# The first layer of a two-layer fp32 trunk in another order: S5 tables between attention projections, the output projection in two halves, a contiguous scan state, softmax scaling on ScalarE

## The chip, the core and the metric

The kernel runs on one NeuronCore of a Trainium2 chip. The metric is the device time of one execution in microseconds. Engines are called by short names: PE is TensorE (matmuls and transposes), DVE is VectorE, ACT is ScalarE, POOL is GpSimd, SP is SyncE, which issues most of the DMAs.

## What is computed

One sequence of L = 256 tokens, D = 2048, all in float32. Two layers share a residual stream. Layer 0 ("even") projects its normed input to q, k, v, u, z_A, z_B of 1024 columns each, runs chunked attention on q, k, v and a state-space model (S5) on u, gates both, and adds their common output projection to x. Layer 1 ("odd") is a causal attention with forget gates; the change does not touch it. The core of layer 0 in the reference:

```python
def even_layer(...):
    hn = rmsnorm(x, norm_g)
    proj = hn @ w_in
    q, k, v, u, z_a, z_b = jnp.split(proj, cuts, axis=-1)
    o_a = chunked_relpos_attention(q.reshape(shp), k.reshape(shp), v.reshape(shp), rel_bias)
    o_a = o_a * jax.nn.silu(z_a)
    y = jax.nn.gelu(s5_ssm(u, lam_re, lam_im, log_dt, b_re, b_im, c_re, c_im, d_skip).astype(x.dtype))
    o_b = y * jax.nn.sigmoid(y @ w_glu + b_glu)
    o_b = o_b * jax.nn.silu(z_b)
    return x + jnp.concatenate([o_a, o_b], axis=-1) @ w_out
```

`s5_ssm` computes, for each of 64 groups of 16 channels, a complex state of 64 numbers, x_t = A x_(t-1) + B u_t, and y_t = Re(C x_t) + D u_t. The attention has 16 heads of 64; with 256 tokens each frame sees its own chunk of 64 and the chunks before it, with a bias by distance.

## The kernel before

**Projections.** Every weight is split on the chip into a float32r high part and the remainder. `next_w` (L117 to L135) loads a 512 KB tile `wr` through SP's queue (4 buffers), ACT rounds it to `wh` (L133), DVE subtracts to `wl` (L134); both have 3 buffers and a scheduling priority 3000 places ahead. `project` (L137 to L158) then does, for each block kb of 128 rows and each half of 128 tokens, three matmuls of 128x512 (L144, L145, L146: high by high, high by low, low by high): 12 matmuls for a weight tile, 96 for a projection of 512 columns over 16 blocks. The weight tiles lie in DRAM in the order in which the program asks for them.

**Order.** The code states dependences and a program order; a scheduler in the framework places the instructions of each engine by priority, and each engine then runs its own list in that order. PE's list in layer 0 is: u0, u1 | zb0, za0, za1 | q0, k0, v0 | q1, k1, v1 | zb1 | glu0, glu1 | oe0 to oe3. Attention runs in two halves (hf) of eight heads: `scores` and `probs` per pair of heads (L552 to L565), mixing with v (L578 to L595).

**S5.** Time is cut into 32 chunks (NCH) of 8 steps (TC). `tables(e)` (L317 to L383) makes, for eight groups e = 0 to 7, the input matrix w1, transposed by PE over `pm` to `min`, the output matrix mx, stored to `m_d`, and the kernel matrix ks, stored to `k_d`. Tables 0 to 2 come before u1, the others after it. `pv`, `vs`, `pvt` (L407 to L422) turn u into chunk inputs in X. The scan (L428 to L433) has 30 steps of four DVE operations on 128 numbers per partition; X is `[P, 2, G, 33]`, so neighbours of a step lie 132 bytes apart. `s5_final` (L500 to L539) loads from `k_d` eight pieces per e into T (five on SP's queue, three on POOL's) and from `m_d` one into mo (SP), in 4 buffers shared with `min`; `py` (L516, L520) multiplies u by T and X by mo, ACT applies GELU into yn (L522), yn goes to DRAM as `y_d` and over `pyt` into yTh and yTl. It stands before v0 in the code. `glu` is a projection over 8 blocks; its result, gated, goes transposed (`out_T`) into blocks 8 to 15 of cTh and cTl, the attention's into blocks 0 to 7; oe0 to oe3 project all 16 and add x.

Of the kernel before, what the change touches and what calls it, by code (L numbers as in the profile page):

```python
# [9 lines left out]
F32 = mybir.dt.float32  # L10
# [32 lines left out]
def trunk(ctx: ExitStack, tc: tile.TileContext, a, out: bass.AP):  # L43
# [120 lines left out]
    l0p = l0.enter_context(tc.tile_pool(name="l0p", bufs=1))  # L164
    s5bx, s5ax = ExitStack(), ExitStack()
# [3 lines left out]
    xt = s5b.tile([P, 2, D], F32, name="xt", tag="X")  # L169
    xr = [s5b.tile([P, 8, L], F32, name=f"xTr_{c}", tag=t_) for c, t_ in enumerate(("un", "uT"))]  # L170
    pre = []

    def x_block(kb):
        src = xr[kb // 8][:, kb % 8, :]
        nc.scalar.activation(xTh[:, kb, :], src, AF.Copy, scale=gE[:, kb:kb + 1])
        nc.vector.scalar_tensor_tensor(xTl[:, kb, :], src, gE[:, kb:kb + 1],
                                       xTh[:, kb, :].bitcast(F32), op0=ALU.mult, op1=ALU.subtract)

    for k0, k1 in ((0, 2), (2, 4), (4, 8), (8, 12), (12, 16)):
        nc.sync.dma_start(xr[k0 // 8][:, k0 % 8:k0 % 8 + k1 - k0, :], a["xT"][:, k0:k1, :])  # L180
# [22 lines left out]
    k_d = dram.tile([NGQ, P, 2 * TC * GC], F32, name="k_d")  # L203
# [3 lines left out]
    uts = []  # L207
    for n in range(2):
        if n == 1:
            pre = [next_w() for _ in range(3)]  # L210
            for t in range(2):
                tc.keep_in_program_order(nc.sync.dma_start(xt[:, t, :], xin[:, t, :]))
                pre += [next_w() for _ in range(2)]
            r0, r0q = rms0(xt)
            pre.append(next_w())
            for t in range(2):
                nc.vector.tensor_scalar(uts[t], uts[t], r0[:, t:t + 1], None, op0=ALU.mult)
                nc.sync.dma_start(u_d[t * P:(t + 1) * P, 0:NT], uts[t])
        acc = project(xTh, xTl, 16, f"u{n}", pre)
        for t in range(2):  # L220
            ut = s5b.tile([P, NT], F32, name=f"ut_{n}_{t}", tag="ut", bufs=3)
            uts.append(ut)
            if n == 0:
                nc.scalar.copy(ut, acc[t])
            else:
                nc.scalar.activation(ut, acc[t], AF.Copy, scale=r0[:, t:t + 1])
                nc.sync.dma_start(u_d[t * P:(t + 1) * P, NT:], ut)
        if n == 0:

            def sm(name):  # L230
                return s5.tile([P, G], F32, name=name, tag="sm_" + name)

            lr, li, dt = sm("lr"), sm("li"), sm("dt")
            for h in range(2):
                nc.gpsimd.dma_start(lr[h * 64:(h + 1) * 64, :], a["s5lr"])
                nc.gpsimd.dma_start(li[h * 64:(h + 1) * 64, :], a["s5li"])
            nc.gpsimd.dma_start(dt, a["s5dt"].to_broadcast([P, G]))
            dcol = s5.tile([P, NGQ], F32, name="dcol")
            nc.gpsimd.dma_start(dcol, a["s5d"])

            sgn = s5.tile([P, 1], F32, name="sgn")
            nc.vector.memset(sgn[0:64, :], -1.0)
            nc.vector.memset(sgn[64:128, :], 1.0)
            nsgn = s5.tile([P, 1], F32, name="nsgn")
            nc.vector.memset(nsgn[0:64, :], 1.0)
            nc.vector.memset(nsgn[64:128, :], -1.0)
            ddiag = s5.tile([P, NGQ, GC], F32, name="ddiag")
            dmask = s5.tile([P, GC], F32, name="dmask")
            for g4 in range(4):
                nc.vector.tensor_copy(dmask[32 * g4:32 * g4 + 32, :],  # L250
                                      ident[32 * g4:32 * g4 + 32, 32 * g4:32 * g4 + GC])
            nc.vector.tensor_tensor(ddiag, dmask.unsqueeze(1).to_broadcast([P, NGQ, GC]),
                                    dcol.unsqueeze(2).to_broadcast([P, NGQ, GC]), op=ALU.mult)

# [48 lines left out]
            V.tensor_tensor(ci, pi[:, 1, :], lr, op=ALU.mult)
            V.tensor_tensor(t0, nr, li, op=ALU.mult)
# [560 lines left out]
```

## Time and profile before

| | us |
|---|---|
| median of three runs | 972.3 |
| lowest and highest | 972.21, 973.33 |
| the profiled execution | 975.55 |
| its span, first to last instruction | 973.5 |
| start of layer 1 (first matmul of cq) | 480.4 |

PE is busy for 941.0 us of the span, DVE for 603.9, ACT for 494.4, POOL for 84.5; the mean granted clock of TensorE is 0.988. In views of the trace L134 is line 134 of the kernel, names of tiles stand without the numbers of their buffers, and "A <- B: 3.3, 3, 2.1" in a list of waits means that A waited for B three times, 3.3 us in all, 2.1 at most. A matmul's printed length includes its way through the array; the distance between two starts is what it costs.

### The profile page before, as it was taken

What the parts mean: (1) busy time and instruction counts of PE and PEld (TensorE: products, weight loads), DVE (VectorE), ACT (ScalarE), POOL (GpSimd) and SP (SyncE); (2) the same over time, 40 slices, a digit from 0 to 9 for tenths busy, and PEclk for the clock granted to TensorE, in tenths of its full rate; (3) what the DMA queues carried; (4) which work ended last, traced back from release to release, by engine and by line L of the source; (5) the groups of instructions that cost most, each with busy time, mean ns of one, the idle gap of its engine ahead of it and who ended that gap; (6) DMA issues with size and microseconds to landing.
All of it is one profiled execution on the core that took longest, in us unless ns stands there. A gap on an engine that the chain in (4) does not pass through costs nothing.

```text
span 973.5 us, 13313 instructions
## 1 busy us (share of the span) xinstructions
PE 941.0 (97%) x4828; PEld 758.7 (78%) x4828; DVE 603.9 (62%) x1095; ACT 494.4 (51%) x730; POOL 84.5 (9%) x142
## 2 busy tenths in 40 slices
PE   7999999999997999999999999999999999999996
PEld 5877887776775786788887888888888888888884
DVE  6899989599832668655546445445544554455463
ACT  6635555445452567444544555456445544554451
POOL 2100000100021010000000320011001100100210
PEclk9999999999997999999999999999999999999998
DMA  8788767755599664556664654555455545554562
GB/s 306 282 246 291 236 206 221 200 167 164 164 244 258 211 204 154 174 199 208 198 223 156 213 194 152 195 174 194 153 193 178 169 158 190 180 170 159 190 207 87
DMA packets 72577, 191.47 MB, mean 197 GB/s; under 512 B 7488, under 2 KB 27184, under 8 KB 72128
## 3 DMA queue, kind: packets, MB, share of 16 engines
q1 hardware_dynamic: 71520, 188.93, 60.5%
q0 software_dynamic: 992, 1.69, 0.9%
q8 instruction: 38, 0.62, 0.3%
q14 instruction: 27, 0.22, 0.1%
HBM read 180.09 MB, written 10.50 MB: 196 GB/s over the span
## 4 chain that ended last, share of the span: by engine, by line
PE 79%; DVE 11%; DMA 5%; issue 3%; ACT 1%; SPq 0%; POOL 0%; POOLq 0%; DVEq 0%; ACTq 0%
DVE wl L134 4%; PE acc_oe L145 3%; PE acc_oe L144 3%; PE acc_oe L146 3%; PE acc_cv L144 3%; PE acc_cq L145 3%; PE acc_cq L146 3%; PE acc_cq L144 3%; PE acc_ck L144 3%; PE acc_cv L145 3%; PE acc_cz L145 3%; PE acc_cz L146 3%; PE acc_cz L144 3%; PE acc_cv L146 3%; PE acc_ck L145 3%; PE acc_ck L146 3%
## 5 line engine op out<-in xcount | busy, mean ns | idle before, releaser
L134 DVE TENSOR_TENSOR wl<-wr,wh 128x1024 fp32r<-128x1024 f32 (+1 forms) x292 | 357.3, 1226 | 286.1 <-ACT wh L133 282.4
L133 ACT ACTIVATE wh<-wr 128x1024 fp32r<-128x1024 f32 (+1 forms) x292 | 307.6, 1056 | 302.8 <-PE acc_ck L146 41.8
L145 PE MATMUL acc_cv<-wl,x1Th 128*128 128x512 f32 x128 | 51.0, 399 | 0.0
L146 PE MATMUL acc_cq<-wh,x1Tl 128*128 128x512 f32 x128 | 50.8, 397 | 0.0
L145 PE MATMUL acc_oe<-wl,cTh 128*128 128x512 f32 x128 | 50.8, 398 | 0.0
L145 PE MATMUL acc_cz<-wl,x1Th 128*128 128x512 f32 x128 | 50.7, 396 | 0.0
L146 PE MATMUL acc_cz<-wh,x1Tl 128*128 128x512 f32 x128 | 50.4, 394 | 0.0
L146 PE MATMUL acc_cv<-wh,x1Tl 128*128 128x512 f32 x128 | 50.4, 393 | 0.0
L145 PE MATMUL acc_cq<-wl,x1Th 128*128 128x512 f32 x128 | 50.3, 393 | 0.0
L145 PE MATMUL acc_ck<-wl,x1Th 128*128 128x512 f32 x128 | 50.2, 392 | 0.0
L146 PE MATMUL acc_oe<-wh,cTl 128*128 128x512 f32 x128 | 50.0, 397 | 0.0
L146 PE MATMUL acc_ck<-wh,x1Tl 128*128 128x512 f32 x128 | 49.9, 390 | 0.0
L144 PE MATMUL acc_cq<-wh,x1Th 128*128 128x512 f32 x128 | 48.5, 398 | 0.0
L144 PE MATMUL acc_cz<-wh,x1Th 128*128 128x512 f32 x128 | 48.3, 402 | 0.0
L144 PE MATMUL acc_oe<-wh,cTh 128*128 128x512 f32 x128 | 48.3, 400 | 0.0
L144 PE MATMUL acc_cv<-wh,x1Th 128*128 128x512 f32 x128 | 47.7, 398 | 0.0
L144 PE MATMUL acc_ck<-wh,x1Th 128*128 128x512 f32 x128 | 46.2, 390 | 0.0
L146 PE MATMUL acc_oo<-wh,oTl 128*128 128x512 f32 x108 | 42.2, 391 | 0.0
L145 PE MATMUL acc_oo<-wl,oTh 128*128 128x512 f32 x108 | 42.1, 390 | 0.0
L144 PE MATMUL acc_oo<-wh,oTh 128*128 128x512 f32 x108 | 39.8, 393 | 0.0
L724 POOL TENSOR_SCALAR cbt<-ckb,cum 128x128 f32<-128x128 f32 x16 | 10.3, 642 | 328.8 <-DVE mx_c L473 271.0
L144 PE MATMUL acc_u<-wh,xTh 128*128 128x512 f32 x64 | 23.8, 412 | 6.3 <-ACT wh L133 6.3
(391 smaller groups left out, 2025.5 us busy)
## 6 DMA issues: line engine op xcount, KB each, us to landing
wr<-in_w_dram SPq DMA_DIRECT2D x295, 512.0 KB, 3.5
m_d<-mx SPq DMA_DIRECT2D x8, 512.0 KB, 4.5
mo<-m_d SPq DMA_DIRECT2D x8, 512.0 KB, 7.0
T<-k_d SPq DMA_DIRECT2D x40, 64.0 KB, 5.6
bc<-in_s5bc_dram SPq DMA_DIRECT2D x8, 256.0 KB, 5.0
xt<-in_x_dram SPq DMA_DIRECT2D x2, 1024.0 KB, 9.4
k_d<-ks SPq DMA_DIRECT2D x8, 256.0 KB, 3.3
bt<-in_rbx_dram SPq DMA_DIRECT2D x8, 256.0 KB, 4.4
```

Source lines behind the costliest of these rows:

```text
L133: nc.scalar.activation(wh[:, c], raw[:, c], AF.Copy)
L134: nc.vector.tensor_tensor(wl[:, c], raw[:, c], wh[:, c].bitcast(F32), op=ALU.subtract)
L144: nc.tensor.matmul(acc[t], sh, wh[:, c], start=kb == 0, stop=False)
L145: nc.tensor.matmul(acc[t], sh, wl[:, c], start=False, stop=False)
L146: nc.tensor.matmul(acc[t], sl, wh[:, c], start=False, stop=kb == nkb - 1)
L724: W.tensor_scalar(bt[:, 0, :], ckb[:, hh, 0:P], cum[:, 0, h:h + 1], None, op0=ALU.add)
```

## The change

1. Layer 0's program order becomes u0, u1, q0, k0, v0, za0, q1, k1, v1, za1, zb0, zb1, with one `tables(e)` and one pair of heads placed after each projection or two. The scan starts behind zb0. The weight tiles in DRAM follow the new order.
2. The output projection is split by its input: oa0 to oa3 (8 blocks, attention half, aTh and aTl) run before the S5 output is complete and add x into tiles xa_n; oe0 to oe3 (8 blocks, S5 half, bTh and bTl) add xa_n at the end.
3. X is `[P, 33, 2, G]`: the 128 numbers of one step are contiguous.
4. In `probs` of layer 0 the scaling by the reciprocal sum and the copy pT go from DVE to ACT; so do the half swaps of vs.
5. Tables: bb and its companion are made in three operations of 256 elements in place of six of 128; slot 0 of w1 and of mx is copied by ACT, DVE computes the other 7 and 8. `k_d` has another layout and is written by four DMAs per e.
6. All loads of T and mo are on POOL's queue, in 7 buffers; `y_d` is written in two halves.

The core of the diff:

```diff
-    X = s5b.tile([P, 2, G, NCH + 1], F32, name="X")
-    nc.gpsimd.memset(X[:, :, :, 0:1], 0.0)
+    X = res.tile([P, NCH + 1, 2, G], F32, name="X", tag="X")
+    nc.gpsimd.memset(X[:, 0], 0.0)
...
+        for n in range(1, NCH - 1):
+            V.tensor_tensor(st2, e2, X[:, n, ::-1, :], op=ALU.mult)
+            V.tensor_tensor(st1, e1, X[:, n], op=ALU.mult)
+            V.tensor_tensor(st2, st2, X[:, n + 1], op=ALU.add)
+            V.tensor_tensor(X[:, n + 1], st1, st2, op=ALU.add)
...
+        V.tensor_tensor(bb, bc[:, :, 0:2, :],
+                        cr[:, sl].unsqueeze(2).unsqueeze(3).to_broadcast([P, 8, 2, GC]), op=ALU.mult)
...
+        nc.scalar.copy(w1[:, :, 0, :], bb[:, :, 0, :])
+        V.tensor_tensor(w1[:, :, 1:8, :], pw(pr, up), wide(bb[:, :, 0, :], 7), op=ALU.mult)
...
-        nc.vector.tensor_copy(vs[:, 1, :, 0:64], pv[:, :, 64:128])
-        nc.vector.tensor_copy(vs[:, 1, :, 64:128], pv[:, :, 0:64])
+        nc.scalar.copy(vs[:, 1, :, 0:64], pv[:, :, 64:128])
+        nc.scalar.copy(vs[:, 1, :, 64:128], pv[:, :, 0:64])
...
-            nc.vector.tensor_scalar(lg[:, 0, :], lg[:, 0, :], rs[:, 0:1], None, op0=ALU.mult)
-            nc.vector.tensor_scalar(lg[:, 1:3, :], lg[:, 1:3, :], rs[:, 1:2], None, op0=ALU.mult)
+            nc.scalar.activation(lg[:, 0, :], lg[:, 0, :], AF.Copy, scale=rs[:, 0:1])
+            nc.scalar.activation(lg[:, 1:3, :], lg[:, 1:3, :], AF.Copy, scale=rs[:, 1:2])
...
-        nc.vector.tensor_copy(pT, pp)
+        if scaled:
+            nc.scalar.copy(pT, pp)
...
-                (nc.gpsimd if j % 8 >= 5 else nc.sync).dma_start(
...
-            nc.sync.dma_start(mo, m_d[e])
+            tt_ = s5c.tile([P, 8, P], F32, name=f"T_{e}", tag="TM", bufs=7)
...
+                nc.gpsimd.dma_start(tt_[j * GC:(j + 1) * GC], k_d[e, :, :, GC * (j + 1):GC * (j + 1) + P])
...
+            nc.gpsimd.dma_start(mo, m_d[e])
...
+    a0.proj("q", r0q)
+    tables(0)
+    a0.proj("k", r0)
+    tables(1)
+    a0.pair(0)
+    a0.proj("v", r0)
+    tables(2)
+    a0.pair(1)
+    a0.gate()
+    tables(3)
...
+    scan()
+    a1.pair(1)
+    a1.mix(0)
+    a1.mix(1)
+    zb.append(gate("zb1"))
+    for hp in (2, 3):
+        a1.pair(hp)
+        a1.mix(hp)
...
+    def out_a(n):
+        t_ = at.tile([P, 2, NT], F32, name=f"xa_{n}", tag=("qk", "qk", "v", "za")[n], bufs=(2, 2, 1, 3)[n])
+        nc.sync.dma_start(t_, xin[:, :, n * NT:(n + 1) * NT])
+        acc = project(aTh, aTl, 8, f"oa{n}")
+        for t in range(2):
+            V.tensor_tensor(t_[:, t, :], acc[t], t_[:, t, :], op=ALU.add)
+        xa.append(t_)
+
+    out_a(0)
+    yns = s5_final()
+    out_a(1)
+    yT = res.tile([P, 2, 8, L], F32R, name="yT", tag="X")
+    s5_y(yns, yT[:, 0], yT[:, 1])
...
-        acc = project(cTh, cTl, 16, f"oe{n}")
...
+        acc = project(bTh, bTl, 8, f"oe{n}")
```

`pair(hp)` is the body of the old loop over pairs of heads (transposes of q and k, scores, `probs`), `mix(i)` the old product with v with og, aTh and aTl, `gate` the old projection with SiLU.

The order of DVE's instructions shows where the scan lies. Before, its steps stand among the weight splits of k0 to k1 and the softmax of the first heads (st1 and st2 are the two temporaries, wl_67 is a weight tile of q1, a2 a head):

```order
L430 TENSOR_TENSOR st2_1235<-e2_431,X_806 128x128
L431 TENSOR_TENSOR st1_1234<-e1t_434,X_806 128x128
L432 TENSOR_TENSOR st2_1235<-st2_1235,X_806 128x128
L134 TENSOR_TENSOR wl_67_2868<-wr_67_2866,wh_67_2867 128x1024
L433 TENSOR_TENSOR X_806<-st1_1234,st2_1235 128x128
L471 ISA lg_a2_2203,mx_a2_2204<-psc_a2_2197,bt_0_1_2194 128x128
```

Now its last steps stand behind the splits of zb1 and of the first part of oa1 (a15 is the last head, og_1_3 the last attention output, xa_0 the sum of oa0 with x, wl_102 the third weight tile of oa1):

```order
L435 TENSOR_TENSOR st1_2896<-e1t_215,X_655 128x128
L482 RECIPROCAL rs_a15_3346<-sm_a15_3343 128x2
L436 TENSOR_TENSOR st2_2897<-st2_2897,X_655 128x128
L437 TENSOR_TENSOR X_655<-st1_2896,st2_2897 128x128
L558 TENSOR_TENSOR og_1_3_3361<-poa_1_3_3356,zaT_1_2510 128x256
L560 TENSOR_TENSOR aTl_107<-og_1_3_3361,aTh_106 128x256
L654 TENSOR_TENSOR xa_0_3365<-acc_oa0_0_3367,xa_0_3365 128x512
L654 TENSOR_TENSOR xa_0_3365<-acc_oa0_1_3368,xa_0_3365 128x512
L134 TENSOR_TENSOR wl_102_3727<-wr_102_3725,wh_102_3726 128x1024
```

The scan moved from the middle of layer 0 to just ahead of the S5 output, and the split wl_102 is queued behind its end. On PE, before, the S5 output is followed by the end of v1 and by zb1 (pyt are the transposes of y, poa the attention outputs of the first half):

```order
L590 MATMUL poa_2_2791<-pT_a_2293,v_2624 64x128
L146 MATMUL acc_v_0_3324<-wh_3453,xTl 128x512
L144 MATMUL acc_v_1_3325<-wh_3453,xTh 128x512
L145 MATMUL acc_v_1_3325<-wl_3454,xTh 128x512
L146 MATMUL acc_v_1_3325<-wh_3453,xTl 128x512
L144 MATMUL acc_zb_0_3508<-wh_3511,xTh 128x512
```

Now py_0 and its neighbours stand between the last head and the end of oa0 (acc_oa_0 and acc_oa_1 are the two token halves):

```order
L488 MATMUL pp_a_3331<-ident,lg_a_3318 128x128 x3
L552 MATMUL poa_3_3356<-pT_a_3335,v_2237 64x256
L608 MATMUL py_3456<-T_3445,uT 32x128 x4
L488 MATMUL pp_a_3350<-ident,lg_a_3337 128x128 x3
L612 MATMUL py_3456<-mo_3454,X 32x128 x4
L608 MATMUL py_3456<-T_3445,uT 32x128 x4
L612 MATMUL py_3456<-mo_3454,X 32x128 x4
```

In PE's list the matmuls with X, which need the scan's end, now stand ahead of the last matmuls of oa0 and of all but the first twelve of oa1. On POOL's queue, before, three pieces of T per e; now eight pieces and mo, one e after the other:

```order
L600 DMA T_2_3503<-k_d_199 16x8x128 x8
L602 DMA mo_2_3512<-m_d_200 128x1024
L600 DMA T_3_3532<-k_d_199 16x8x128 x8
L535 MEMSET bt_1_3_3309 64x2x64
L602 DMA mo_3_3541<-m_d_200 128x1024
L600 DMA T_4_3561<-k_d_199 16x8x128 x8
L602 DMA mo_4_3570<-m_d_200 128x1024
```

mo_3 takes the buffer of T_0, T_4 that of mo_0, and so on, so they wait until py_0 is done.

More of the change, by code (lines that the diff above doesn't have):

```diff
@@ L402, in trunk, with sm @@
-    X = s5b.tile([P, 2, G, NCH + 1], F32, name="X")
-    nc.gpsimd.memset(X[:, :, :, 0:1], 0.0)
-    for e in range(8):
-        if e >= NE_EARLY:
-            tables(e)
+    def sm(name):
+        return s5.tile([P, G], F32, name=name, tag="sm_" + name)
+    lr, li, dt = sm("lr"), sm("li"), sm("dt")
+    pr = s5.tile([P, 9, G], F32, name="pr")
+    pi = s5.tile([P, 9, G], F32, name="pi")
+    psg = s5.tile([P, 9, G], F32, name="psg")
+    sgn = s5.tile([P, 1], F32, name="sgn")
+    nsgn = s5.tile([P, 1], F32, name="nsgn")
@@ L437, in trunk @@
-    zb = l0p.tile([P, 2, 2 * NT], F32, name="zb")
-    zaT = l0p.tile([P, 8, L], F32, name="zaT")
-    def gate(z_, nm, n):
-        acc = project(xTh, xTl, 16, f"{nm}{n}")
-        for t in range(2):
-            nc.scalar.activation(z_[:, t, n * NT:(n + 1) * NT], acc[t], AF.Silu, scale=r0[:, t:t + 1])
-    gate(zb, "zb", 0)
-    for n in range(2):
+            nc.scalar.copy(X[:, 1:, w, e * 8:e * 8 + 8],
+                           pt[:, w].rearrange("p k (g n) -> p n (k g)", n=NCH))
+    us = []
@@ new lines, in trunk @@
+    for n in range(2):
+        if n == 1:
+            pre = [next_w() for _ in range(3)]
+            xt = res.tile([P, 2, D], F32, name="xt", tag="X")
+            for t in range(2):
+                tc.keep_in_program_order(nc.sync.dma_start(xt[:, t, :], xin[:, t, :]))
+                pre += [next_w() for _ in range(2)]
+            r0, r0q = rms0(xt)
+            pre.append(next_w())
+            for t in range(2):
+                V.tensor_scalar(us[0][:, t, :], us[0][:, t, :], r0[:, t:t + 1], None, op0=ALU.mult)
+                nc.sync.dma_start(u_d[t * P:(t + 1) * P, 0:NT], us[0][:, t, :])
+        acc = project(xTh, xTl, 16, f"u{n}", pre)
+        ut = at.tile([P, 2, NT], F32, name=f"ut_{n}", tag="qk")
+        us.append(ut)
+        for t in range(2):
+            if n == 0:
+                nc.scalar.copy(ut[:, t, :], acc[t])
+            else:
+                nc.scalar.activation(ut[:, t, :], acc[t], AF.Copy, scale=r0[:, t:t + 1])
+                nc.sync.dma_start(u_d[t * P:(t + 1) * P, NT:], ut[:, t, :])
+        if n == 0:
+            s5_setup()
@@ L446, in trunk, with gate, gate_T @@
+    def gate(name):
+        z_ = at.tile([P, 2, NT], F32, name=name, tag="za", bufs=3)
+        acc = project(xTh, xTl, 16, name)
+        for t in range(2):
+            nc.scalar.activation(z_[:, t, :], acc[t], AF.Silu, scale=r0[:, t:t + 1])
+        return z_
+    def gate_T(n):
+        zaT = at.tile([P, 4, L], F32, name=f"zaT_{n}", tag="za", bufs=3)
         acc = project(xTh, xTl, 16, f"za{n}")
         for t in range(2):
-            zt = s5b.tile([P, NT], F32, name=f"za_{n}_{t}", tag="ut", bufs=3)
+            zt = at.tile([P, NT], F32, name=f"za_{n}_{t}", tag="qkT")
@@ new lines, in trunk, with __init__, proj, gate @@
+    class Half:
+        def __init__(self, hf):
+            self.hf, self.work = hf, []
+        def proj(self, w, scale):
+            dst = at.tile([P, 2, NT], F32, name=f"{w}_{self.hf}", tag="v" if w == "v" else "qk",
+                          bufs=1 if w == "v" else 2)
+            acc = project(xTh, xTl, 16, f"{w}{self.hf}")
+            for t in range(2):
+                nc.scalar.activation(dst[:, t, :], acc[t], AF.Copy, scale=scale[:, t:t + 1])
+            setattr(self, w, dst)
+        def gate(self):
+            self.zaT = gate_T(self.hf)
+        def pair(self, hp):
+            hf = self.hf
@@ new lines, in mix @@
+            nc.scalar.copy(aTh[:, kb, :], og)
+            V.tensor_tensor(aTl[:, kb, :], og, aTh[:, kb, :].bitcast(F32), op=ALU.subtract)
+    zb = []
+    a0, a1 = Half(0), Half(1)
+    a0.proj("q", r0q)
[8 more added lines that the diff above has]
+    tables(3)
+    a0.mix(0)
+    a0.mix(1)
+    for hp in (2, 3):
+        a0.pair(hp)
+        a0.mix(hp)
+    a1.proj("q", r0q)
+    tables(4)
+    a1.proj("k", r0)
@@ new lines, in s5_y, with dst @@
+    def s5_y(yns, yTh, yTl):
+        for hh in range(2):
+            for ih in range(2):
+                py = ps_tr.tile([P, 4, P], F32, name=f"pyt_{hh}_{ih}", tag="tr")
+                for k in range(4):
+                    nc.tensor.transpose(py[:, k, :], yns[hh][:, ih * 4 + k, :], ident)
+                src = py.rearrange("p i (g n) -> p g n i", n=NCH)
+                def dst(t_):
+                    return (t_.rearrange("p (g h) (n i) -> p h g n i", h=2, i=TC)
+                            [:, hh, :, :, ih * 4:ih * 4 + 4])
+                nc.scalar.copy(dst(yTh), src)
+                V.tensor_tensor(dst(yTl), src, dst(yTh).bitcast(F32), op=ALU.subtract)
```

519 lines of the change are left out of this document (231 added, 288 removed).

## The prediction

> **What bounds the kernel now.** I read the page first: TensorE (PE) is at work nearly all the time, VectorE (DVE) much less on average.
>
> ```profile
> PE 941.0 (97%) x4828; PEld 758.7 (78%) x4828; DVE 603.9 (62%) x1095; ACT 494.4 (51%) x730; POOL 84.5 (9%) x142
> ```
>
> Layer 1 does not change, so only the first 480 us count, and of them only what PE loses there. The list of PE's waits, ordered by cost, gives the losses (us in total, times, longest):
>
> ```profile
> PE acc_u L144 <- ACT wh L133: 6.3, 1, 6.3
> PE py L520 <- DMA mo<-m_d: 3.3, 3, 2.1
> PE acc_zb L145 <- DVE wl L134: 2.3, 1, 2.3
> PE pm L368 <- DVE w L354: 1.9, 1, 1.9
> PE py L516 <- DMA T<-k_d: 1.6, 1, 1.6
> PE acc_q L145 <- DVE wl L134: 1.6, 3, 0.7
> PE acc_k L145 <- DVE wl L134: 1.2, 2, 0.8
> PE acc_v L145 <- DVE wl L134: 0.9, 3, 0.4
> PE acc_glu L144 <- DVE ob L611: 0.8, 1, 0.8
> ```
>
> The first line is the start-up, which no edit shortens. The other eight are 3.3 + 2.3 + 1.9 + 1.6 + 1.6 + 1.2 + 0.9 + 0.8 = 13.6 us. The second loss is clock. The table by stage gives PE, PEld, DVE, ACT and POOL busy, then the granted clock, the share of the DMA engines and GB/s:
>
> ```profile
> 60.00:80.00 20.00, 20.00 (x98) 15.78 (x98) 18.92 (x25) 8.50 (x14) 0.31 (x1) 0.91 0.93 299
> 160.00:180.00 20.00, 16.64 (x144) 12.38 (x143) 10.07 (x18) 8.77 (x19) 4.24 (x10) 0.91 0.81 225
> 181.00:254.00 73.00, 70.43 (x330) 54.94 (x329) 71.68 (x179) 36.20 (x54) 0.43 (x2) 1.00 0.54 169
> 277.00:320.00 43.00, 37.96 (x314) 27.97 (x313) 12.89 (x13) 13.00 (x17) 6.92 (x14) 0.88 1.04 249
> 600.00:640.00 40.00, 40.00 (x180) 33.00 (x179) 17.37 (x15) 18.89 (x20) 0.00 (x0) 1.00 0.57 186
> ```
>
> Three rows run below full clock: 0.09 x 20 + 0.09 x 20 + 0.12 x 43 = 8.8 us. Together 13.6 + 8.8 = 22.4 us: the most that a better order of layer 0 can give back. Row 181:254 is the scan: DVE is busy 71.68 of 73 us and PE still gets 70.43, since more than three projections (96 x 0.227 = 21.8 us each, by the matmul rows below) run beside it. Row 277:320 is the S5 output: DMA is saturated (1.04) while the T and mo tables come in. Row 600:640 is layer 1 undisturbed.
>
> **The change, part by part.** Prices on DVE (groups by line: behind the first bar busy us and the mean ns of one):
>
> ```profile
> L134 DVE TENSOR_TENSOR wl<-wr,wh 128x1024 fp32r<-128x1024 f32 x138 | 168.6, 1226 | 93.9 <-ACT wh L133 92.0 <-DMA T<-k_d 1.5
> L360 DVE TENSOR_TENSOR tm<-pi,cc 128x1152 f32<-128x1152 f32 x8 | 10.8, 1349 | 0.3 <-ACT cc L340 0.3
> L353 DVE TENSOR_TENSOR tw<-psg,bw 128x1024 f32<-128x1024 f32 x8 | 9.7, 1216 | 0.0
> L489 DVE COPY pT_a<-pp_a 128x384 f32<-128x384 f32 x16 | 8.4, 548 | 1.4 <-PE pp_a L487 0.9 <-PE poa L590 0.5
> L473 DVE CUSTOM_DVE_ANT_0 lg_a<-psc_a,bt 128x256 f32<-128x256 f32 x16 | 6.7, 418 | 0.0
> L484 DVE TENSOR_SCALAR lg_a<-lg_a,rs_a 128x256 f32<-128x256 f32 x16 | 5.6, 351 | 0.0
> L625 DVE TENSOR_TENSOR xr<-acc_oe,xr 128x512 f32<-128x512 f32 x8 | 5.1, 682 | 0.0
> L483 DVE TENSOR_SCALAR lg_a<-lg_a,rs_a 128x128 f32<-128x128 f32 x16 | 4.8, 301 | 0.4
> L471 DVE CUSTOM_DVE_ANT_0 lg_a<-psc_a,bt 128x128 f32<-128x128 f32 x16 | 4.5, 284 | 0.9 <-PE psc_a L464 0.9
> L593 DVE TENSOR_TENSOR og<-poa,zaT 128x256 f32<-128x256 f32 x8 | 3.3, 417 | 1.4 <-PE poa L590 1.4
> L476 DVE TENSOR_SCALAR nm_a<-mx_a 128x2 f32<-128x2 f32 x16 | 2.4, 165 | 0.0
> L336 DVE TENSOR_TENSOR bw<-bc,cr 128x128 f32<-128x128 f32 x8 | 2.2, 280 | 0.0
> ```
>
> One scan step on the timeline of DVE (start, length):
>
> ```profile
> 192.69 0.40 DVE L430 TENSOR_TENSOR st<-e,X 128x128 f32<-128x128 f32 x1
> 193.00 0.39 DVE L431 TENSOR_TENSOR st<-e1t,X 128x128 f32<-128x128 f32 x1
> 193.31 0.40 DVE L432 TENSOR_TENSOR st<-st,X 128x128 f32<-128x128 f32 x1
> 193.74 0.40 DVE L433 TENSOR_TENSOR X<-st,st 128x128 f32<-128x128 f32 x1
> ```
>
> *DVE relief.* An operation starts 0.31 us after an independent one and 0.43 after one that it needs: a step is 0.31 + 0.43 + 0.43 + 0.31 = 1.48 us. Of the same 128 elements, L336 takes 0.28 instead of 0.40. I take four such savings of 0.115 per step (the truth lies between none and that): 1.02 us, 30 steps, 13.9 us saved. Tables: six operations of 128 become three of 256, 6 x 0.28 - 3 x 0.42 = 0.4; w1 loses an eighth, 3 x 1.216 / 8 = 0.46; mx goes from 1152 elements to 1024, 3 x 0.133 = 0.4; eight times 1.26 are 10 us. Softmax scale and pT copy: 5.6 + 4.8 + 8.4 = 18.8. The half swaps of vs, at L336's length, 16 x 0.28 = 4.5. The new adds of xa cost 8 x 0.68 = 5.5. Net about 42 us of DVE go, most of them to ACT, which was busy 36.20 of 73 us in the scan stage and has room. None of it is time on PE by itself: it counts where DVE bounds.
>
> *Order.* I give the new order credit for all 22.4 us: DVE no longer feeds tables and projections at 95%, and the early T and mo loads stop meeting q, k and v. New losses come against it, six of them.
>
> 1. Start-up: two bias loads of 256 KB now stand before the fourth weight tile. At 299 GB/s they take 1.75 us, of which I charge 0.6 since the bc loads move the other way (ends 0 and 1.75).
>
> 2. Tables among attention projections: PE still waits for pm and pv now and then; I take 2, ends 1 and 4, from the 1.9 of the pm row.
>
> 3. The tail of the scan, the largest. In DVE's new order, between the splits wl_100 and wl_102, stand 41 scan operations, two splits, softmax of four heads, two og, two aTl and two xa adds. PE needs wl_102 for the second half of oa1. DVE's sum: 41 x 0.255 = 10.5; 2 x 1.23 = 2.5; 4 x (0.284 + 0.418) = 2.8; eight small ones at 0.165 = 1.3; 4 x 0.42 = 1.7; 2 x 0.68 = 1.4: 20.2. DVE also stands still while the last pair goes through exp, scaling, transposes, the pT copy and the output product on other engines; these two rows of ACT show two of the hops:
>
> ```profile
> L479 ACT ACTIVATE lg_a<-lg_a,nm_a 128x256 f32<-128x256 f32 x16 | 7.9, 494 | 0.0
> L522 ACT ACTIVATE yn<-py 128x256 f32<-128x256 f32 x8 | 3.1, 384 | 13.5 <-PE py L520 13.3
> ```
>
> About ten hops near 0.5 are 5 us, together 25. For that time PE has 46 matmuls of projections, the last scores and py_0 to py_3. A matmul takes the array 0.23 us:
>
> ```profile
> 604.65 0.39 PE L144 MATMUL acc_cq<-wh,x1Th 128*128 128x512 f32 x1
> 604.88 0.39 PE L145 MATMUL acc_cq<-wl,x1Th 128*128 128x512 f32 x1
> ```
>
> 46 x 0.23 = 10.6, and with 4 to 5 for the rest 15. Loss 25 - 15 = 10. Without the hops, and with a little queued ahead, it is 4.4; with slower steps 13. zb1, which could have filled the gap, stands before it.
>
> 4. Clock after those gaps: by the 0.88 row, 0.12 x 25 = 3 (ends 0 and 5). The Trainium skill, page "TensorE: Matmul & The Clock Gate", section "HAM oscillation — how this bites in real kernels", says that an idle gap of more than about 3.4 us drops the array to half rate and a shorter one doesn't. By that rule one long gap would cost about half of 3.4 us, 1.7 (an estimate from that page), and the sum below would end 1.3 us lower.
>
> 5. After py_7: GELU 0.38, two transposes, cast and subtraction at about 0.6 each, before glu0 can run past its first four matmuls: 2.5 (ends 1 and 4); before, projections covered this.
>
> 6. T and mo. These rows are of stage 277:320 alone (median us to landing at the end):
>
> ```profile
> wr<-in_w_dram SPq DMA_DIRECT2D x11, 512.0 KB, 7.8
> mo<-m_d SPq DMA_DIRECT2D x5, 512.0 KB, 7.8
> T<-k_d SPq DMA_DIRECT2D x20, 64.0 KB, 7.9
> T<-k_d POOLq DMA_DIRECT2D x14, 64.0 KB, 7.9
> ```
>
> With seven buffers, mo_3 and everything behind it waits for py_0: 37 loads, on POOL's queue alone, which has eight in flight at most. At 7.9 that is 37 / 8 x 7.9 = 36.5 us, against 132 matmuls x 0.23 = 30 plus 4 for py and transposes = 34 us of PE work from py_3 to py_7. I charge 2 (ends 0 and 5).
>
> Losses: 0.6 + 2 + 10 + 3 + 2.5 + 2 = 20.1. Gain 22.4 - 20.1 = 2.3 us. The profiled execution took 975.55 us (span 973.5 and 2 around it), 3.25 above the median of 972.3; I subtract the gain from both: 973.3 profiled, **970.0** as median.
>
> **The rivals.**
>
> *The tail is covered* (chance 0.14). The saved 42 us of DVE let the splits run ahead, the tail costs its 4.4, the tables 1, the clock 1: 0.6 + 1 + 4.4 + 1 + 2.5 + 0.5 = 10, gain 12.4, 960. For it: in row 181:254 PE lost only 2.57 us with DVE at 98%. Against: that stretch had more than three projections beside it, the tail has half a one.
>
> *It cancels* (0.19): waits and clock come back in full elsewhere, 972.3. For it speaks that 20.1 lies within one term's ends of 22.4.
>
> *One queue for T and mo* (0.17), the case of the other sign. Landings took up to
>
> ```profile
> DMA to landing us min/median/max: 2.4/5.9/10.2
> ```
>
> At 10.2 the 37 loads take 47.2 us, 13 more than PE's 34 instead of my 2: 970 + 11 = 981. It decides from 34 x 8 / 37 = 7.4 us per landing. Against: the 16 engines carry fewer transfers at that place than in 277:320. The Trainium skill, page "DMA: Bandwidth & Descriptors", section "Issuing engine by pattern", holds loads issued by SyncE to be generally faster than those by GpSimd. The trace agrees only weakly: 7.9 on either queue under load.
>
> *The scan is no faster* (0.16). If 0.40 per operation is not a matter of the stride, the step stays at 1.48 and the tail takes the 13.9: 984. For it: the dependent start of 0.43 is longer than the operation of 0.40. Against: L336 at 0.28.
>
> My forecast has 0.34.
>
> **How the numbers follow.** A measurement of this kernel can tell about 0.2% (1.9 us) from no change: faster is below 970.4, slower above 974.2. Forecast and the covered tail are faster, 0.34 + 0.14 = 0.48; same 0.19; slower 0.17 + 0.16 = 0.33. The forecast's own range is 964 to 975 by the ends of the terms. For 8 in 10 the range takes in the covered tail from 958 and the slow queue to 982; beyond lie most of the scan's case and a little on either side.
>
> **What would show it.** Right: scan operations of about 0.28 us; no PE wait on wl in q, k and v; one stretch of some 25 us after zb1 with DVE full and PE short by about 10; the clock below 1 only there; py_4 to py_7 waiting little for T and mo. Wrong: scan operations still at 0.40; PE waits on T or mo of over 5 us in all; waits on pm, pv or wl among the attention projections above 4 us; the tail short by under 5.

## The result and the profile after

The changed kernel takes 977.72 us (median of seven runs, 976.73 to 983.51) against 973.19 us for the kernel before (970.72 to 975.56): a ratio of 1.0057, 95% interval 1.0033 to 1.0081. It is slower by 4.5 us where I forecast 2.3 us faster. The time lies inside the range and above the 974.2 from which I called it slower. A second set (run e1 below) gives 1.0041, interval 1.0026 to 1.0056.

The profiled execution of the changed kernel took 976.73 us (span 975.0), the lowest of its seven times; that of the kernel before took 975.55, near the top of its seven. The two profiles lie 1.2 us apart, so they show where the time sits, not the whole 4.5 us. Layer 1 starts at 481.2 instead of 480.4.

PE's waits after the change:

```profile
PE acc_u L144 <- ACT wh L133: 6.3, 1, 6.3
PE py L612 <- DMA mo<-m_d: 2.7, 2, 2.0
PE pu L424 <- ACT un L421: 2.3, 1, 2.3
PE py L608 <- DMA T<-k_d: 2.2, 1, 2.2
PE acc_u L145 <- DVE wl L134: 1.1, 2, 0.6
PE acc_oa L145 <- DVE wl L134: 0.9, 1, 0.9
PE acc_oe L144 <- ACT wh L133: 0.9, 1, 0.9
PE poa L552 <- ACT pT_a L491: 0.8, 1, 0.8
```

The waits on wl in q, k and v (3.7 us before, about 1 now) and on w in the tables are nearly gone, as forecast. The waits for mo and T stand there as before: 2.7 + 2.2 = 4.9 us, the same sum as 3.3 + 1.6. New is pu, the transposes of u, which wait for u's way to DRAM and back. The table by stage (PE, PEld, DVE, ACT, POOL busy, clock, DMA share, GB/s):

```profile
60.00:80.00 20.00, 17.39 (x77) 13.74 (x76) 10.55 (x14) 10.04 (x19) 0.21 (x1) 0.91 0.71 233
340.00:360.00 20.00, 16.89 (x155) 10.64 (x153) 13.91 (x61) 13.01 (x35) 4.83 (x9) 1.00 0.52 157
360.00:380.00 20.00, 20.00 (x150) 15.96 (x149) 10.20 (x10) 8.56 (x10) 9.21 (x18) 1.00 1.06 267
380.00:400.00 20.00, 17.88 (x128) 13.11 (x126) 10.15 (x10) 7.08 (x9) 6.02 (x11) 1.00 1.03 256
400.00:420.00 20.00, 16.69 (x89) 12.86 (x90) 8.61 (x8) 5.79 (x10) 6.84 (x2) 0.83 0.75 241
```

Three places lose time: 60 to 80 (u), 340 to 360 (end of the scan, last heads) and 380 to 420 (T and mo, then the chain into glu0). At 340 to 360 the DMA engines are half idle, right after it they are full. The scan itself did what the change says; one step on DVE's timeline:

```profile
344.15 0.29 DVE L434 TENSOR_TENSOR st<-e,X 128x128 f32<-128x128 f32 x1
344.37 0.28 DVE L435 TENSOR_TENSOR st<-e1t,X 128x128 f32<-128x128 f32 x1
344.57 0.28 DVE L436 TENSOR_TENSOR st<-st,X 128x128 f32<-128x128 f32 x1
344.88 0.29 DVE L437 TENSOR_TENSOR X<-st,st 128x128 f32<-128x128 f32 x1
345.21 0.29 DVE L434 TENSOR_TENSOR st<-e,X 128x128 f32<-128x128 f32 x1
```

From 344.15 to 345.21 are 1.06 us (1.48 before).

To compare stages I made a ledger from PE's timeline. For each instruction it takes the distance to the next start, less the usual step: 0.227 us for a 512-column matmul, for the small ones the lower quartile of their distances in the profile before. What is left is wait, low clock or a poor sequence. It begins with the first matmul, at 6.3 us.

| us from the start | before | changed | what stands there in the changed kernel |
|---|---|---|---|
| 0 to 60 | 6.5 | 3.6 | start, u0, u1 |
| 60 to 160 | 5.6 | 12.0 | q0, k0, v0, tables 0 to 3 |
| 160 to 180 | 7.1 | 1.0 | (before: table chain) |
| 180 to 280 | 9.4 | 8.1 | q1 to za1, tables 4 to 7 |
| 280 to 320 | 11.7 | 1.4 | zb0, zb1 (before: S5 output) |
| 320 to 360 | 1.6 | 9.0 | last heads, end of the scan |
| 360 to 420 | 6.0 | 12.1 | oa1 to oa3, py_4 to py_7, glu0 |
| 420 to 480 | 1.8 | 3.9 | glu1, oe |
| sum | 49.7 | 51.1 | |

The losses moved from 160 to 180 and 280 to 320 to three other places and kept their sum.

### The profile page after: what moved, and what is told of

The parts are those of the page before. It is cut to its first block, busy times and chain, and to the rows that moved or that the text cites. A ratio compares the mean times of both kernels' runs of the same rounds, so it can differ in the third digit from the quotient of the medians.

```text
span 975.0 us, 13264 instructions
## 1 busy us (share of the span) xinstructions
PE 944.1 (97%) x4828; PEld 758.1 (78%) x4828; DVE 575.2 (59%) x1015; ACT 515.8 (53%) x810; POOL 106.6 (11%) x176
## 4 chain that ended last, share of the span: by engine, by line
PE 83%; DMA 6%; DVE 5%; issue 3%; ACT 2%; SPq 0%; POOLq 0%; POOL 0%; DVEq 0%; ACTq 0%
PE acc_cv L144 3%; PE acc_cq L146 3%; PE acc_cq L145 3%; PE acc_cq L144 3%; PE acc_ck L144 3%; PE acc_cz L144 3%; PE acc_cz L146 3%; PE acc_cz L145 3%; PE acc_cv L145 3%; PE acc_cv L146 3%; PE acc_ck L145 3%; PE acc_ck L146 3%; PE acc_oo L145 3%; PE acc_oo L144 3%; PE acc_oo L146 3%
## 5 line engine op out<-in xcount | busy, mean ns | idle before, releaser
L145 PE MATMUL acc_cv<-wl,x1Th 128*128 128x512 f32 x128 | 51.1, 399 | 0.0
L795 POOL TENSOR_SCALAR cbt<-ckb,cum 128x128 f32<-128x128 f32 x16 | 10.2, 637 | 328.4 <-DVE mx_c L474 270.9
L600 POOL DMA_DIRECT2D T<-k_d x64 | 34.1, 538 | 41.9 <-DMA T<-k_d 16.1
L144 PEld LDWEIGHTS acc_cv<-wh,x1Th 128*128 128x128 f32 x128 | 24.1, 188 | 5.4 <-issue 0.4
L144 PEld LDWEIGHTS acc_ck<-wh,x1Th 128*128 128x128 f32 x128 | 24.0, 188 | 5.0
```

Of the source, the lines that this page charges most:

```text
L144: nc.tensor.matmul(acc[t], sh, wh[:, c], start=kb == 0, stop=False)
L145: nc.tensor.matmul(acc[t], sh, wl[:, c], start=False, stop=False)
L600: nc.gpsimd.dma_start(tt_[j * GC:(j + 1) * GC], k_d[e, :, :, GC * (j + 1):GC * (j + 1) + P])
L795: W.tensor_scalar(bt[:, 0, :], ckb[:, hh, 0:P], cum[:, 0, h:h + 1], None, op0=ALU.add)
```

## The experiments

Each was timed in several runs against the kernel before on the same chip; differences to the changed kernel are taken to e1, 978.9. Four chips were used: the kernel before took 974.0 on that of e1 to e4, 974.7 on that of e5 to e8, 976.0 on that of e9 to e11 and 975.0 on that of e12 and e13. By these medians e9, e10 and e11 are 2 us nearer to e1 than the differences below say, and e5, e6, e7 and e13 about 1 us faster.

**e1, the changed kernel again.**

> The changed kernel once more, nothing altered: the yardstick for the other runs on the same chip. Every theory: 976.5 to 979.5 us, 3 to 6 us over the kernel before. Its profile should again show PE losing about 8 us where the scan ends (340 to 360 us) and about 10 us where the last T and mo tables come in (380 to 420).

978.89 us, ratio 1.0041 (1.0026 to 1.0056). In its ledger 320 to 360 holds 8.8 and 360 to 420 holds 12.8: the two places are stable.

**e2, the old queues for T and mo.**

```diff
-                nc.gpsimd.dma_start(tt_[j * GC:(j + 1) * GC], k_d[e, :, :, GC * (j + 1):GC * (j + 1) + P])
+                (nc.gpsimd if j % 8 >= 5 else nc.sync).dma_start(tt_[j * GC:(j + 1) * GC], k_d[e, :, :, GC * (j + 1):GC * (j + 1) + P])
...
-            nc.gpsimd.dma_start(mo, m_d[e])
+            nc.sync.dma_start(mo, m_d[e])
```

> The changed kernel with T and mo loads on the queues of before: five of eight pieces of T and mo on SP, three pieces on POOL. Queue theory (eight loads in flight on one queue are the limit): landings fall from 8 us, PE's waits for T and mo (4.9 us) go, 3 to 5 us faster than the changed kernel. Saturation theory (the 16 DMA engines are full at a share of 1.03, whoever issues): within 1.5 us of the changed kernel, landings as long as before.

987.29 us, 8.4 slower than e1, which neither theory gave. PE's waits for T and mo stay:

```profile
PE py L612 <- DMA mo<-m_d: 3.8, 2, 3.0
PE pu L424 <- ACT un L421: 3.4, 1, 3.4
PE py L608 <- DMA T<-k_d: 2.4, 1, 2.4
PE acc_zb L144 <- ACT wh L133: 1.7, 2, 0.9
```

Neither theory holds as put. The 37 loads behind py_0 do pass faster, in 25.5 us (366.4 to 391.9) where e1 takes 49.2 (356.5 to 405.7). But the DMA share stays at 0.98, and one weight tile is loaded beside them instead of 13: the weights stand on SP's queue behind T and mo. The first half of the tables delays them too (acc_zb waits). At 300 to 340 the splits wait for wh, first in e1, then in e2 (behind the first bar busy us and mean ns, behind the second the idle time before them):

```profile
L134 DVE TENSOR_TENSOR wl<-wr,wh 128x1024 fp32r<-128x1024 f32 x13 | 15.9, 1224 | 2.5 <-ACT wh L133 2.4
L134 DVE TENSOR_TENSOR wl<-wr,wh 128x1024 fp32r<-128x1024 f32 x11 | 13.5, 1223 | 11.2 <-ACT wh L133 11.2
```

The scan stands in the same list of DVE and ends at 365.5 instead of 355.3, and py_0 follows it. Moving the loads to POOL, which I had made the rival on the slow side, helped the new order.

**e3, zb1 behind oa0**, as cover for the end of the scan.

```diff
-    zb.append(gate("zb1"))
...
     yns = s5_final()
+    zb.append(gate("zb1"))
     out_a(1)
...
+    parts += [tiles(wout[:D // 2], 0, 1), tiles(we, zb + 1, zb + 2), tiles(wout[:D // 2], 1, 4), tiles(f["w_glu"][0], 0, 2), tiles(wout[D // 2:], 0, 4)]
```

> The changed kernel with zb1 moved from ahead of the last two pairs of heads to behind oa0, so that 96 matmuls stand beside the end of the scan. Tail theory (DVE's scan and softmax leave PE without work): the 8 us lost at 340 to 360 shrink to 2 or 3, 5 to 7 us faster than the changed kernel. Table theory (T and mo of the second half, which wait for py_0, are the larger cost): at most 2 us faster, since those loads still start behind py_0.

981.59 us, 2.7 slower than e1: both theories missed. By stage:

```profile
320.00:340.00 20.00, 15.74 (x81) 8.98 (x80) 17.91 (x82) 10.96 (x33) 3.22 (x7) 1.00 0.57 165
380.00:400.00 20.00, 20.00 (x141) 15.25 (x140) 8.87 (x9) 6.65 (x8) 7.13 (x14) 1.00 1.04 261
400.00:420.00 20.00, 18.13 (x107) 13.72 (x106) 11.49 (x12) 8.65 (x12) 1.65 (x1) 1.00 0.88 260
```

zb1 now covers the table loads: PE's waits for T and mo are gone from the list and the ledger's 360 to 420 falls from 12.8 to 7.1. The stage of the heads and the scan, which has lost zb1, costs 13.8 at 300 to 340. One projection was moved from one hole to the other.

**e4, the old scan state in the new order.**

```diff
-    X = res.tile([P, NCH + 1, 2, G], F32, name="X", tag="X")
+    X = res.tile([P, 2, G, NCH + 1], F32, name="X", tag="X")
...
-            V.tensor_tensor(X[:, n + 1], st1, st2, op=ALU.add)
+            V.tensor_tensor(X[:, :, :, n + 1], st1, st2, op=ALU.add)
```

> The changed kernel with the scan state laid out as before (neighbours 132 bytes apart). A step goes from 1.06 us back to 1.48, 30 steps cost 12.6 us more of DVE. Tail theory: DVE sets the end of the scan, so 8 to 13 us slower than the changed kernel. If the scan ends with time to spare: 0 to 2 us slower.

988.18 us, 9.3 slower: with 12.6 us more for DVE the scan's end does set the time.

**e5, T and mo loaded for three e only** (the tables of the other five are left out; y uses the three again).

```diff
+            if e < 3:
...
+                kept.append((tt_, mo))
+            tt_, mo = kept[e % 3]
```

> The changed kernel, but T and mo are loaded for e = 0, 1, 2 only and used again for e = 3 to 7: 45 of 72 loads and their 5 MB are left out, y is computed with the wrong tables. Table theory (the loads behind py_0 keep PE waiting and hold up the chain from py_7 to glu0): PE's waits on T and mo go, the 10 us lost at 380 to 420 fall to 4, 5 to 7 us faster than the changed kernel. Tail theory alone: under 2 us faster.

967.29 us, 11.6 faster than e1. The stage that lost most is whole:

```profile
380.00:400.00 20.00, 20.00 (x91) 16.53 (x90) 12.65 (x12) 8.03 (x8) 5.57 (x2) 1.00 0.75 250
400.00:420.00 20.00, 20.00 (x90) 16.22 (x90) 12.88 (x14) 9.87 (x10) 0.00 (x0) 1.00 0.55 179
```

The ledger's 360 to 420 falls from 12.8 to 2.3. The table theory holds, by more than I gave it: in the new order the loads of the last five e cost about 11 us, and with them the clock and the chain into glu0.

**e6, ten scan steps of thirty** (the other twenty are left out).

```diff
-        for n in range(1, NCH - 1):
+        for n in range(1, 11):
```

> The changed kernel with 10 of the 30 scan steps; the other 20 are left out. 21 us of DVE go. Tail theory (the scan's DVE time is what PE waits for): the 8 us lost at 340 to 360 fall to about 3, where the last pairs of heads still run one after the other, 4 to 6 us faster. If the chain of the heads sets that loss by itself: 0 to 2 us faster.

975.49 us, 3.4 faster. But not where the tail theory says:

```profile
340.00:360.00 20.00, 16.75 (x135) 10.94 (x137) 6.69 (x30) 12.94 (x35) 3.19 (x6) 1.00 0.54 164
380.00:400.00 20.00, 20.00 (x139) 15.27 (x138) 9.70 (x9) 7.13 (x8) 6.08 (x11) 1.00 1.03 281
```

DVE at 340 to 360 falls from 13.91 to 6.69 us busy, and PE stays at 16.75 (16.89 in the changed kernel). The scan ends at 321.1, and still py_0's first matmul with X starts at 354.9 (355.4 in e1), since the last heads stand ahead of it. So DVE's sum by itself is not that loss. What the shorter scan gives comes at 360 to 420, where the ledger falls from 12.8 to 6.2.

**e7, a third order**: tables(7) ahead of za1, all pairs of heads ahead of zb0, zb1 behind the S5 output.

```diff
     tables(6)
-    a1.pair(0)
-    a1.gate()
     tables(7)
+    a1.gate()
+    a1.pair(0)
+    a1.mix(0)
+    for hp in (1, 2, 3):
+        a1.pair(hp)
+        a1.mix(hp)
```

> The changed kernel in a third order: table 7 ahead of za1, so that the scan can start under za1 and zb0; all pairs of heads of the second half ahead of zb0; zb1 behind the S5 output as cover for T and mo. Tail theory: the scan ends before PE needs it, 6 to 10 us faster than the changed kernel. Chain theory (what run e3 suggests: the pairs of heads cost PE 8 to 10 us wherever they stand with little beside them): the T and mo waits go, the loss at the heads stays, 0 to 4 us faster.

982.33 us, 3.4 slower than e1. Again the table waits go and the heads cost more, 21.8 in the ledger at 300 to 360. The tail theory falls here; the chain theory had the sign wrong in the sum but the place right.

**e8, the old order with DVE's relief alone**: contiguous X, softmax scaling and the pT copy on ACT.

```diff
-    X = s5b.tile([P, 2, G, NCH + 1], F32, name="X")
+    X = s5b.tile([P, NCH + 1, 2, G], F32, name="X")
...
-            nc.vector.tensor_scalar(lg[:, 0, :], lg[:, 0, :], rs[:, 0:1], None, op0=ALU.mult)
+            nc.scalar.activation(lg[:, 0, :], lg[:, 0, :], AF.Copy, scale=rs[:, 0:1])
...
-        nc.vector.tensor_copy(pT, pp)
+        if scaled:
+            nc.scalar.copy(pT, pp)
```

> The kernel before, in its old order, with only the contiguous scan state and the softmax scaling and pT copy on ACT: 13 us and 19 us less for DVE. Order theory (DVE relief counts only where DVE bounds, and in the old order it bounds little): 0 to 3 us faster than before, the gain being the waits on wl in q, k and v (3.7 us). Relief theory (DVE at 98% in the scan's stage is the bound): 5 to 10 us faster than before.

970.36 us against 974.69 for the kernel before, ratio 0.9957 (0.9942 to 0.9973). It beats both kernels. The stages of before, now:

```profile
181.00:254.00 73.00, 71.85 (x346) 57.77 (x345) 59.42 (x176) 43.52 (x78) 0.59 (x3) 1.00 0.59 188
277.00:320.00 43.00, 38.88 (x310) 29.61 (x309) 14.52 (x14) 15.54 (x21) 5.77 (x12) 0.96 1.02 268
```

DVE falls from 71.68 to 59.42 of 73 us and PE's shortfall from 2.57 to 1.15. A gain of 4 us lies a little above what the order theory gave.

**e9, the eight T loads of an e as one.**

```diff
-            for j in range(TC):
-                nc.gpsimd.dma_start(tt_[j * GC:(j + 1) * GC], k_d[e, :, :, GC * (j + 1):GC * (j + 1) + P])
+            ke = k_d[e, :, :, GC:GC + P]
+            nc.gpsimd.dma_start(tt_, bass.AP(ke.tensor, ke.offset, [[GC, TC]] + list(ke.ap)))
```

> The changed kernel with the eight T loads of an e made as one DMA of 512 KB over the same bytes: POOL issues 16 loads in place of 72, so eight in flight reach over four e. Queue theory (eight small loads in flight, one by one as they land, are the limit): PE's waits on T and mo go, 5 to 10 us faster than the changed kernel. Saturation theory (the 16 engines are full with pieces of 512 bytes whoever issues them): 0 to 2 us faster.

988.91 us, 10 slower (8 by the kernel before on the same chip). Loads and landings in 280 to 420, first of e9, then of the changed kernel (280 to 410):

```profile
wr<-in_w_dram SPq DMA_DIRECT2D x32, 512.0 KB, 5.4
T<-k_d POOLq DMA_DIRECT2D x8, 512.0 KB, 19.6
mo<-m_d POOLq DMA_DIRECT2D x8, 512.0 KB, 17.2
```

```profile
wr<-in_w_dram SPq DMA_DIRECT2D x33, 512.0 KB, 8.2
T<-k_d POOLq DMA_DIRECT2D x64, 64.0 KB, 8.0
mo<-m_d POOLq DMA_DIRECT2D x8, 512.0 KB, 8.6
```

These stretches are long, and most of the weight loads in them have no table beside them. While the tables behind py_0 come in (364.2 to 400.2 in e9, 354.9 to 403.2 in the changed kernel), the weights land in 25.6 us instead of 10.2:

```profile
wr<-in_w_dram SPq DMA_DIRECT2D x4, 512.0 KB, 25.6
wr<-in_w_dram SPq DMA_DIRECT2D x13, 512.0 KB, 10.2
```

Each table load takes 17 to 20 us, yet these tables pass in 36.0 us instead of 48.3, and the weights pay for it: the DMA share is 1.00 in the one stretch and 1.01 in the other. Neither theory holds, and what the limit of eight costs by itself stays open. The trace shows where the time went. At 300 to 340 the splits wait 9.9 us for wh (2.4 in e1), the scan ends at 363.0 instead of 355.3, and py_0 and the loads behind it start that much later.

**e10, the new order without the relief** (old X, scaling and pT on DVE).

> The changed kernel without its relief of DVE: scan state as before, softmax scaling and pT copy on DVE. What is left is the new order, the split output projection and the table edits. If order and relief simply add (relief was 4 us in the old order): 983. If the new order needs the relief because the scan and the heads stand at its end (the old scan state alone cost 9 us): 990 to 998.

994.1 us, ratio 1.0186 (1.0172 to 1.02). Order, split and table edits alone cost 18 us, the relief returns 13 to 15 of them; in the old order the same relief is worth 4. They do not add.

**e11, pu held back behind q0.**

```diff
+        V.tensor_scalar(one, a0.q[:, 0, 0:1], 0.0, 1.0, op0=ALU.mult, op1=ALU.add)
...
-        nc.scalar.copy(un4, un[:, ::-1, b * 64:(b + 1) * 64].rearrange("p j (k c) -> p k j c", c=GC))
+            nc.scalar.activation(un4, un[:, ::-1, b * 64:(b + 1) * 64].rearrange("p j (k c) -> p k j c", c=GC),
+                                 AF.Copy, scale=one)
```

> The changed kernel with the copies un4 scaled by a 1 that is computed from q0, so that the transposes pu come behind q0 on PE's list and not inside it. Round-trip theory (u goes to DRAM and back with one projection as cover; PE waits 2.3 to 3.4 us for pu and the clock drops to 0.91 after it, 5 us at 60 to 80): 2 to 4 us faster than the changed kernel. If the tables behind it then come late in turn: 0 to 1.

985.72 us, 6.8 slower (5 by the kernel before on the same chip); neither theory. ACT's timeline shows the next wait behind the one that was moved:

```profile
65.09 1.06 ACT L133 ACTIVATE wh<-wr 128x1024 fp32r<-128x1024 f32 x1 [3.95 <-DMA wr<-in_w_dram]
74.69 0.40 ACT L322 ACTIVATE bc<-bc,nsgn 128x128 f32<-128x128 f32 x1 [8.54 <-DMA bc<-in_s5bc_dram]
75.00 0.29 ACT L323 ACTIVATE bc<-bc 128x128 f32<-128x128 f32 x1
75.20 1.04 ACT L133 ACTIVATE wh<-wr 128x1024 fp32r<-128x1024 f32 x1
```

ACT stands 8.54 us for the table inputs bc, with the rounding of the next weights behind it, and PE waits 5.4 us for wh. The start of the new order hangs on several loads at once; what u's round trip costs by itself stays open.

**e12, T and mo loaded for two e only, in the kernel before** (the tables of the other six are left out; y uses the two again).

> The kernel before, but T and mo are loaded for e = 0 and 1 only and used again for the others: 54 of 72 loads and their 6 MB are left out, y is computed with the wrong tables. It prices the loads in the old order. If the old order paid for them as much as the new one does (11.6 us): 9 to 12 us faster than before. If it hid them better, as the waits (4.9) and the clock (5.2) of that stage allow at the least: 5 to 8. If it hid them wholly: 0 to 2.

961.93 us against 974.97, 13.0 faster by the medians (ratio of the runs 0.9851, 0.9832 to 0.9871). The stage that had DMA share 1.04 and clock 0.88:

```profile
277.00:320.00 43.00, 43.00 (x332) 33.48 (x330) 24.23 (x44) 22.65 (x38) 3.02 (x2) 1.00 0.61 180
```

The old order paid for these loads what the new one pays: 13.0 for six e left out, 11.6 for five.

**e13, the last two pairs of heads without scores and softmax** (the first two pairs' probabilities are used again).

> The changed kernel without the last two pairs of heads: their scores and softmax are left out and the probabilities of the first two pairs used again in the products with v. Chain theory (each pair goes PE, ACT, PE, DVE, ACT, PE, ACT, PE in turn, with nothing beside it): the 8 us lost at 340 to 360 fall to 2 or less. DVE theory (the scan and the splits by themselves hold PE up there): 5 or more stay. The time as a whole falls by up to 10 us, less if the tables then come later against PE's list.

979.88 us, no faster; but by stage:

```profile
340.00:360.00 20.00, 20.00 (x100) 15.74 (x100) 19.62 (x52) 8.69 (x9) 0.00 (x0) 1.00 0.75 240
380.00:400.00 20.00, 8.91 (x92) 6.43 (x90) 5.36 (x5) 2.90 (x5) 10.87 (x21) 0.75 0.93 238
```

At 340 to 360 PE is full while DVE is busier (19.62) than in the changed kernel (13.91), as the chain theory says. But the scheduler put py later in this version, most of it behind oa2, so other matmuls stand at that place, and the scan ends only at 366.5. The run does not show by itself that the heads were the cost. The wait for T and mo at 380 to 420 took back what that stage had given.

## Why the prediction was wrong, step by step

**The credit of 22.4 us** was the step that failed: "I give the new order credit for all 22.4 us". Of these, 3.3 + 1.6 of waits and 0.12 x 43 = 5.2 of clock, 10.1 in all, belonged to T and mo. They were no matter of the order. The bytes have to pass engines that are then full (share 1.04 before, 1.03 to 1.06 after), and e12 and e5 price the loads that they leave out at 13.0 and 11.6 us. I saw the row with 1.04, read it as a meeting with q, k and v that the new place would avoid, and charged 2 us for T and mo and 2.5 for the chain after py_7. Net I had forecast 10.1 - 4.5 = 5.6 us of gain there; the removal runs leave 1.4, which lies within their intervals, and e12 left out one e more. Another 4.1 us of the credit (2.3 of acc_zb's wait, 1.8 of clock at 60 to 80) came back close by, as pu's wait of 2.3 with the clock at 0.91. So 14.2 of the 22.4 us stayed.

The rows tell why the new place is no better. With seven buffers POOL loads T_0 to T_3 early and then stands until py_0 has freed them, which needs the scan's end:

```profile
325.51 0.20 POOL L535 MEMSET bt<- 64x128 f32 x1 [2.30 <-DMA bt<-in_rbx_dram]
354.92 0.57 POOL L602 DMA_DIRECT2D mo<-m_d  x1 [29.21 <-PE py L612]
```

For 29 us POOL issues no table load, and at 340 to 360 the DMA share falls to 0.52; then half of all tables must come between 355 and 403, beside the weights:

```profile
354.90:403.20 48.30, 42.73 (x352) 32.28 (x351) 22.60 (x23) 17.94 (x22) 20.07 (x37) 1.00 1.01 264
```

My sum of 36.5 against 34 us, charged with 2, had the right loads and the right sign and was too small: the 37 loads took 48.3 us. It left out that 13 weight tiles share the full engines at that place. In e2 the same loads pass in 25.5 us, with one weight tile beside them.

**The tail** was priced at 10 + 3 of clock; the ledger shows 9.0 at 320 to 360 (1.6 before), and the clock row there reads 1.00. The size was near; the mechanism was half of it. I summed DVE's 20.2 us, added ten hops as 5 more, and set 15 us of PE's against the sum. The trace shows two chains that end together. One is DVE's list: from 340 to the scan's end its longest idle is 0.35 us, and py_0's first matmul with X starts 0.1 us behind the last operation of the scan:

```profile
353.45 0.29 DVE L437 TENSOR_TENSOR X<-st,st 128x128 f32<-128x128 f32 x1
353.84 0.54 PE L612 MATMUL py<-mo,X 128*32 128x128 f32 x8
```

The other is one pair of heads at a time going to and fro between PE, ACT and DVE, as PE's timeline shows:

```profile
349.81 0.63 PE L146 MATMUL acc_oa<-wh,aTl 128*128 128x512 f32 x2
350.74 0.84 PE L488 MATMUL pp_a<-ident,lg_a 128*128 128x128 f32 x3 [0.31 <-ACT lg_a L484]
352.38 0.43 PE L552 MATMUL poa<-pT_a,v 128*64 128x256 f32 x1 [0.80 <-ACT pT_a L491]
```

Three transposes and one product spread over 2.5 us, each behind ACT. The hops do not come on top of DVE's sum; they take as long beside it. The traces of the variants (us from the start):

| run | scan ends | py_0's first matmul with X | layer 1 starts |
|---|---|---|---|
| e1 | 355.3 | 355.4 | 483.4 |
| e2 | 365.5 | 365.6 | 492.3 |
| e4 | 364.7 | 364.8 | 493.2 |
| e9 | 363.0 | 363.1 | 494.1 |
| e11 | 364.6 | 365.2 | 493.1 |
| e6 | 321.1 | 354.9 | 477.1 |

In the first five py_0 goes within 0.6 us of the scan's end, and layer 1 starts 127 to 131 us behind it: what delays the scan delays the kernel. In e6 the heads hold py_0 at the same place. A shorter scan alone therefore gains little there; whether a shorter scan and fewer heads together would, no run shows.

The 3 us of clock came in another place, 400 to 420: 0.17 x 20 = 3.4. The Trainium skill's rule that an idle gap of more than about 3.4 us throttles the array ("TensorE: Matmul & The Clock Gate", section "HAM oscillation — how this bites in real kernels") does fit the stage at 340 to 360, where the longest gap was 0.9 us and the clock held. It does not fit 400 to 420, where no wait was longer than 2.2 us and the clock still fell to 0.83, nor 60 to 80, with one wait of 2.3 us and 0.91.

**The start of attention.** 60 to 160 rose from 5.6 to 12.0 us; I had 2 for the tables and nothing for u. Before, pu stood at 113 us on PE's list behind two projections; now it stands inside q0, where PE comes to it at 68 us and waits 2.3 us, with a clock of 0.91 around it. I listed PE's new order and did not ask of each moved step how far its load lies behind it. e11 did not get the time back.

**DVE's relief** was right for the scan: 1.06 us a step (1.02 forecast), about 0.285 us an operation. The total of 42 us was too high: by the two profiles DVE's busy time falls from 603.9 to 575.2 us, by 28.7. "None of it is time on PE by itself: it counts where DVE bounds" held in its second half. In the old order it was worth 4 us (e8); in the new one, where DVE is busy for 49.6 of the 53.7 us from 300 to the scan's end, the kernel would take 994 without it.

**The sum.** With 14.2 of the credit taken back, the tail at 9.0 instead of 13, and the 4.5 for T, mo and the chain dropped, since their whole 10.1 stays, my terms give 8.2 - (0.6 + 2 + 9.0) = -3.4 us, against -4.5 measured. This is a reckoning after the fact, not a proof. That the tail was charged too high hid part of the error in the credit: a piece of luck. The forecast's own range of 964 to 975 was also too narrow: the ends of its terms, added up, give 956 to 982.

**The rivals.** One queue for T and mo had the place (py_4 to py_7) and the sign right, and its 47.2 us for the 37 loads lie near the 48.3 measured. Its reason, landings of 10.2 us on one queue, was not right: they landed in 8.4 us in the median, and e2 and e9 show that tables and weights share full engines whichever queue issues them. Its 981 is the nearest of the five times to the median of 977.72. The covered tail did not come; e3 and e7 show why: there was one spare projection for two holes. The cancelling case came nearest to the profiles, where the ledger's sums are 49.7 and 51.1. The case of an unchanged scan fell with 0.285 us an operation.

## What to carry to other kernels

A wait on a load is credited to a new order only after asking whether the DMA engines are full at that place; where the share is 1.0, the bytes have a price wherever they go, and the run that leaves the loads out gives it. Find the instruction that releases the loads (here py_0, behind the scan) and what it waits for. A reorder moves cover as well as work: list the stages that need something beside them (here a serial softmax, a round trip through DRAM, a burst of tables) and count the independent projections that are left for each. Relief of an engine and a new order are to be timed apart: here the relief alone made the faster kernel.

## What the runs showed of the hardware

With full engines, table loads of 64 KB landed in 8.0 us, at most eight in flight on POOL's queue; made as loads of 512 KB in pieces of the same size they took 19.6, the weight loads beside them took 25.6 instead of 10.2, and the program was 8 to 10 us slower. The same DVE operation on 128 elements takes 0.40 us with neighbours 132 bytes apart and 0.285 us contiguous. The granted clock fell after single waits of PE of 2.3 us, to 0.66 over 60 to 65 in the kernel before and to 0.67 over 70 to 75 in the changed one, and to 0.83 over 400 to 420, where waits of 2.2 and 2.0 us stood close together. It stayed at 1.00 at 340 to 360, with as much idle time in pieces of at most 0.9 us.
